# A planner's price list: changes of TensorE tile size, overlapping tiles and a shared port

## The chip, the cores and the metric

The kernel runs on one core of a Trainium2 chip. The metric is the device time of one execution in microseconds (us). Before the change three runs took 1749.36, 1751.22 and 1751.43 us. TensorE does matmuls (PE; its weight loads are PEld), VectorE (DVE), ScalarE (ACT) and GpSimd (POOL) work on elements, SyncE (SP) issues the DMAs that bring the weights.

## What is computed

A sequence of 256 tokens with 1024 features passes a first block and then a second block of two layers. In fp32, cut to what matters:

```
mod = silu(c) @ w_ada + b_ada                        # shift, scale and gate of a sublayer
h = rms_norm(x) * (1 + scale) + shift
first block, mixer:   p = h @ w_in
   y_a = rwkv7(r, decay, k, v, kk, a)                # 12 heads of 64: state' = state * w - (state kk)(kk a) + v k
   y_b = dilated window attention, three groups      # 12 heads of 64
   x += gate * rms_norm((sig(p_ga) * y_a @ w_a + sig(p_gb) * y_b @ w_b) @ w_out)
feed-forward:         x += gate * (silu(h @ w_u) * (h @ w_g)) @ w_o
second block, mixer (twice): compressed, selected and window attention (8 heads), forgetting
   attention (4 heads), attention within a block (4 heads), one output projection
order: mixer1, ffn, ffn, mixer2, ffn, ffn, mixer2, ffn, final norm
```

## The kernel before

**Dense products.** Features lie on the partitions, tokens on the free axis. A weight is loaded as fp32 in pieces of 128x1024 (`raw`), and split into two exact float32r parts: ACT writes `hi`, DVE writes `lo = raw - hi`. The operand is split alike (`hh`, `hl`). A product is three matmuls of 128x128 weights by 256 columns, hi by hh, hi by hl, lo by hh (`mm3`). These are the records `ps_mm<-hh,hi` and so on; a name `out<-a,b` gives the moving operand a and the stationary one b.

**Small products.** The mixers have plain fp32 matmuls with fewer than 128 rows or columns. They use a part of the array: 32x32, 64x64, 128x64 (128 rows, 64 columns), 64x128 or 128x32. An fp32 matmul is two records in the trace. In the first mixer, `rwkv` (L1653) treats two heads at a time, six pairs in three streams with PSUM tiles `ps_a`, `ps_b`, `ps_c`. A pair inverts small triangular blocks with 32x32 products (`block_inverse`, L1829), runs a chain over four chunks of 64 tokens (products `sv,am`, `rs,w`, `sv,c`, `bk,fbk`), and then adds up its output:

```
for n in range(4):
    for h in range(2):
        o = half[h]
        self.mm(py[o, 64 * n:64 * n + 64], sv[:, n, h], am[:, n, h, 1], n == 0, False)
        self.mm(py[o, 64 * n:64 * n + 64], uv[o, n, h], gb[o, n], False, True)
```

The first is the record pair `am,sv`, tile 128x64; the second is `gb,bk`, tile 64x64. Sums into `py` may change places, except that the first of a sum stays first. The norm of `py` follows, with products by exact matrices (`sph,exact`, `spl,exact`), then a gate. The attention (`attend`, L1962; `dilated`, L1613) has score products of 64 rows, transposes and value products of 64 columns.

**Order of the work.** The order is not written by hand. Each call of an engine in a stretch of the program only records an `_Op` with its operands and a duration (`time`, L641; `record`, L660; this helper is why all trace lines are L663). At the end of a stretch, `emit` (L836) plans: `solve` builds the dependencies, `run` (L423) simulates the engines and lets each take the ready instruction with the highest priority, `back` does it from the end to get new priorities, up to four times, and `replay` and `score` judge a plan by its mean end with eight shifts of the clock and noise. The best plan's order is emitted, and each engine keeps it, the DMA issues on SP too. Stretches are: the start (to about 97 us), the first mixer's projection and recurrence (97 to about 360), gates and dilated attention, the output projection, and then one for each feed-forward sublayer and each mixer of the second block.

For TensorE the plan has a price for each matmul, a factor of 2 while its own clock rule says slow, and a reserve: while a tick of that rule is short of columns, dense products go first. POOL and DVE are independent in the plan. The planning is done on the host while the program is built.

Of the kernel before, what the change touches and what calls it, by code (L numbers as in the profile page):

```python
# [25 lines left out]
D = 1024  # L26
# [10 lines left out]
# ---------------------------------------------------------------- host layout  # L37
def _pairs(w, chunks):
    """[K, N] -> [n pairs, 128, (K/128) * 256]: two 128-column chunks per pair, K-chunk major."""
    k = w.shape[0] // 128  # L40
    out = np.empty((len(chunks), 128, k, 256), w.dtype)
    for i, (a, b) in enumerate(chunks):
        out[i, :, :, :128] = w[:, a:a + 128].reshape(k, 128, 128).transpose(1, 0, 2)
        out[i, :, :, 128:] = w[:, b:b + 128].reshape(k, 128, 128).transpose(1, 0, 2)
    return out.reshape(len(chunks), 128, k * 256)


def _rows(w):
    """[K, N] -> [128, K/128, N]"""
    return np.ascontiguousarray(w.reshape(-1, 128, w.shape[1]).transpose(1, 0, 2))  # L50
# [22 lines left out]
# order of the 128-column chunks of the first block's projection  # L73
# [8 lines left out]
# units of the projection whose sums are all kept at a time  # L82
# [4 lines left out]
# order of the head dimensions of the first block's q and k: a rotated pair stays within 32 partitions  # L87
# [3 lines left out]
def _constants():  # L91
# [8 lines left out]
    # first block  # L100
# [60 lines left out]
def _pack(i):  # L161
    f = {k: np.asarray(v) for k, v in i.items()}
    o = {}
# [31 lines left out]
    # first block: six units whose K-chunks come first, then the others  # L195
# [21 lines left out]
    # second block  # L217
# [37 lines left out]
# ---------------------------------------------------------------- order of instructions  # L255
class _Op:
    """an instruction of a stretch of the program whose order is worked out before it is emitted"""
    __slots__ = ("eng", "emit", "cost", "lag", "cols", "tile", "pred", "succ", "prio", "behind", "where", "late", "side", "sums", "real", "start", "left", "ready", "num", "group", "banks")

    def __init__(self, eng, emit, cost, lag):  # L260
        self.eng, self.emit, self.cost, self.lag = eng, emit, cost, lag
        self.pred, self.behind, self.real, self.cols, self.tile, self.ready, self.sums, self.side = {}, [], None, 0.0, None, 0.0, False, False


class _Stretch:
    """the instructions of a stretch, by their dependencies and the times they take: each engine takes what is
    ready, the one with the longest way to the end first. Emission is in that order, and the engines keep it."""
    ENGINES = "pe", "act", "dve", "pool", "dma"
    # from the end of one engine's instruction to the start of another's that waits for it
    LAG = dict(zip(ENGINES, ((0.0, 0.2, 0.22, 0.22, 1.22), (0.24, 0.145, 0.145, 0.18, 1.22), (0.2, 0.13, 0.127, 0.2, 1.22),  # L270
                             (0.2, 0.08, 0.08, 0.1, 1.22), (0.95, 0.95, 0.95, 0.95, 0.0))))
    TICK, COLS = 10.24 / 3, float(2960)

    def __init__(self, model):
# [3 lines left out]
        self.state = dict(dict.fromkeys(self.ENGINES, 2.3), dma=1.69, queue=1.21), (0, 0.0, False, (0.0, None))  # L278
# [52 lines left out]
    def solve(self):  # L331
        ops = self.ops
        # a tile waits for the one whose place it takes
# [8 lines left out]
        # tiles of a ring start in turn  # L342
# [13 lines left out]
        # longest way to the end  # L356
# [13 lines left out]
    def tail(self, o):  # L370
        """us that an instruction without successors may come after the end"""
        return 20 if o.group == 12 else o.late

    def back(self, key):
        """the same from the end backwards: the times left to the end at which the instructions start"""
# [11 lines left out]
        while True:  # L387
# [22 lines left out]
            cost = o.cost  # L410
            if e == "pe":
                if o.side:
                    cost = 0.027
            free[e] = f = t + cost
# [8 lines left out]
    def run(self, prio, margin):  # L423
# [6 lines left out]
        ready = {e: [] for e in engines}        # by priority  # L430
        wait = {e: [] for e in engines}         # by time
        dense = []                              # those of the tensor engine that keep its clock up
# [7 lines left out]
        tick, cols, warm, last = self.state[1]  # L440
        while True:
            best = None
            for e in engines:
                w, t = wait[e], free[e]
                while w and w[0][0] <= t:
                    n = heappop(w)[1]
                    heappush(dense if rich[n] else ready[e], (prio[n], n))
                if not ready[e] and not (e == "pe" and dense):
                    if not w:
                        continue  # L450
                    t = w[0][0]
                if best is None or t < best[0]:
                    best = t, e
            if best is None:
                return end, out, (free, (tick, cols, warm, last))
            t, e = best
            w, r = wait[e], ready[e]
            if not r and not (e == "pe" and dense):
                while w and w[0][0] <= t:
                    n = heappop(w)[1]  # L460
                    heappush(dense if rich[n] else r, (prio[n], n))
            if e == "pe":
                k = int(t / self.TICK)
                if k != tick:
                    tick, warm, cols = k, k == tick + 1 and cols >= self.COLS, 0.0
                short = cols < target and ((k + 1) * self.TICK - t) * 2350 < target - cols + margin
                n = None
                if last[1] is not None and t < last[0] + 0.01 and r and 0:
                    # what the free rows or columns of the array can take at the same time
                    c = [x for x in r if ops[x[1]].tile is not None and not last[1] & ops[x[1]].tile]  # L470
                    if c:
                        c = min(c)
                        n = c[1]
                        r.remove(c)
                        heapify(r)
                if n is None:
                    n = heappop(dense if dense and (not r or short or dense[0] < r[0]) else r)[1]
            else:
                n = heappop(r)[1]
# [12 lines left out]
            if e == "pe":  # L492
                cols += o.cols
                if o.side:
                    cost = 0.027
# [6 lines left out]
            free[e] = f = t + cost  # L502
# [10 lines left out]
    def replay(self, order, phase, noise):  # L513
        """when a schedule ends if the windows of the tensor engine's clock lie otherwise and instructions take longer"""
        free, (tick, cols, warm, last) = dict(self.state[0]), self.state[1]
        tick, at, end = int((free["pe"] + phase) / self.TICK), [o.ready for o in self.ops], 0.0
        read = {}
        for _, n, o, _ in order:
# [7 lines left out]
            if e == "pe":  # L526
                k = int((t + phase) / self.TICK)
                if k != tick:
                    tick, warm, cols = k, k == tick + 1 and cols >= 2950.0, 0.0
                cols += o.cols  # L530
                if o.side:
                    cost = 0.027
                else:
# [1877 lines left out]
```

## Time and profile before

| | |
|---|---|
| three runs, us | 1749.36, 1751.22, 1751.43 (median 1751.22) |
| span of the profiled execution, first to last instruction | 1749.4 us |
| time of the runs beyond that span (median less span) | 1.8 us |
| PE busy | 1658.9 us, 95% of the span |
| DVE, ACT, POOL busy | 1274.3, 910.0, 409.5 us |
| mean granted clock of TensorE | 0.969 of full speed |

The time of the profiled execution itself is its span and what little lies around it; the runs were timed apart from it. In the tables of stretches each line gives the length, then for each engine its busy time and in brackets its instructions, then PEclk, the granted TensorE clock (1.00 is 2.4 GHz, 0.50 is 1.2 GHz), the DMA share and the GB/s. A busy PE is not PE at its peak: a product may hold it long.

### The profile page before, as it was taken

The numbers are of one execution on the slowest core, as the hardware profiler recorded it, in microseconds if no ns is written. First come the engines' busy times: TensorE is split into PE (matmuls) and PEld (weight loads), VectorE is DVE, ScalarE is ACT, GpSimd is POOL, SyncE is SP. The second block draws the span as 40 slices with busy tenths as digits, with TensorE's granted clock in tenths as the row PEclk, the third lists the DMA queues.
The fourth block names the chain that finished last, engine by engine and source line by source line (L and its number), as shares of the span: only waits on it lengthen the run. The fifth ranks groups of instructions, "written<-read, shape, count | busy, mean of one in ns | idle before, by whom it ended". The sixth has DMA issues, their size and how long they took to land.

```text
span 1749.4 us, 35779 instructions
## 1 busy us (share of the span) xinstructions
PE 1658.9 (95%) x14110; PEld 1545.0 (88%) x14110; DVE 1274.3 (73%) x2389; ACT 910.0 (52%) x1707; POOL 409.5 (23%) x486
## 2 busy tenths in 40 slices
PE   5888988999999999999999999999999989999998
PEld 4877777788899999999878799999999977799997
DVE  5697476358877789878787877777777786775553
ACT  4464364357644446454566564545444556565442
POOL 3475053013500024000433330004000414440002
PEclk9989979899999999999999999999999999899999
DMA  9433324235588885878751568896888752245553
GB/s 352 170 123 122 110 75 168 91 127 185 191 274 290 298 294 193 298 276 311 254 177 61 174 201 294 278 309 212 275 293 294 278 194 88 73 157 182 193 181 97
DMA packets 102554, 359.18 MB, mean 205 GB/s; under 512 B 11377, under 2 KB 12913, under 8 KB 102386
## 3 DMA queue, kind: packets, MB, share of 16 engines
q1 hardware_dynamic: 102386, 356.90, 59.9%
q8 instruction: 110, 1.80, 0.4%
q14 instruction: 58, 0.48, 0.1%
HBM read 355.81 MB, written 1.05 MB: 204 GB/s over the span
## 4 chain that ended last, share of the span: by engine, by line
PE 74%; DVE 9%; POOL 4%; issue 2%; ACT 2%; DMA 2%; DVEq 0%; POOLq 0%; SPq 0%; ACTq 0%
PE ps_mm L663 57%; PE ps_a L663 9%; PE ps_b L663 5%; PE ps_c L663 4%; DVE lo L663 3%; POOL fg L663 2%; DMA raw<-in_ada 1%; DVE junk L663 1%; ACT hi L663 1%; DMA w<-in_cw 1%; DVE x L663 0%; DVE rt L663 0%; DVE am L663 0%; ACT w L663 0%; POOL P1a L663 0%
## 5 line engine op out<-in xcount | busy, mean ns | idle before, releaser
L663 DVE TENSOR_TENSOR lo<-raw,hi 128x1024 fp32r<-128x1024 f32 (+2 forms) x478 | 579.8, 1233 | 186.4 <-issue 67.3
L663 ACT ACTIVATE hi<-raw 128x1024 fp32r<-128x1024 f32 (+2 forms) x478 | 487.4, 1025 | 362.2 <-PE ps_mm L663 267.5
L663 PE MATMUL ps_mm<-hh,hi 128*128 128x256 f32 x2040 | 514.7, 289 | 30.0 <-ACT hh L663 18.2
L663 PE MATMUL ps_mm<-hl,hi 128*128 128x256 f32 x2040 | 506.7, 287 | 0.5 <-DVE hl L663 0.4
L663 PEld LDWEIGHTS ps_mm<-hh,hi 128*128 128x128 f32 x2040 | 389.2, 194 | 41.5 <-ACT hh L663 21.2
L663 PEld LDWEIGHTS ps_mm<-hl,hi 128*128 128x128 f32 x2040 | 388.4, 194 | 5.3 <-issue 2.5
L663 PE MATMUL ps_mm<-hh,lo 128*128 128x256 f32 x2040 | 319.3, 285 | 0.7 <-DVE lo L663 0.7
L663 DVE CUSTOM_DVE_ANT_0 junk<-raw,cond 128x1024 bf16<-128x1024 f32 x192 | 241.4, 1257 | 65.3 <-DMA raw<-in_ada 64.0
L663 PEld LDWEIGHTS ps_mm<-hh,lo 128*128 128x128 f32 x2040 | 275.5, 192 | 4.5 <-DVE lo L663 1.3
L663 POOL TENSOR_TENSOR acc<-acc,sq 128x256 f32<-128x256 f32 x46 | 49.7, 1080 | 864.8 <-ACT sq L663 863.2
L663 PE MATMUL ps_mm<-fh,hi 128*128 128x256 f32 x770 | 189.5, 282 | 0.1
L663 PEld LDWEIGHTS ps_mm<-fh,hi 128*128 128x128 f32 x770 | 146.4, 191 | 1.1 <-DVE fy L663 1.1
L663 PE MATMUL ps_mm<-fl,hi 128*128 128x256 f32 x490 | 120.8, 281 | 0.0
L663 PE MATMUL ps_mm<-fh,lo 128*128 128x256 f32 x770 | 115.8, 281 | 0.0
L663 PEld LDWEIGHTS ps_mm<-fh,lo 128*128 128x128 f32 x770 | 102.7, 191 | 0.0
L663 PEld LDWEIGHTS ps_mm<-fl,hi 128*128 128x128 f32 x490 | 93.3, 190 | 0.0
L663 ACT ACTIVATE fh<-fy 128x256 fp32r<-128x256 f32 x110 | 44.9, 411 | 58.7 <-DVE fy L663 58.7
L663 PE MATMUL ps_mm<-fg,hi 128*128 128x256 f32 x280 | 69.7, 281 | 0.0
L663 ACT ACTIVATE su<-ps_mm 128x256 f32<-128x256 f32 x95 | 36.0, 379 | 59.5 <-PE ps_mm L663 59.4
L663 PE MATMUL ps_a<-UH,hi 128*128 128x258 f32 x168 | 50.7, 305 | 4.4 <-ACT UH L663 4.4
L663 ACT ACTIVATE UH<-x,mod 128x256 fp32r<-128x256 f32 x56 | 27.7, 504 | 49.8 <-DVE x L663 49.8
L663 PEld LDWEIGHTS ps_mm<-fg,hi 128*128 128x128 f32 x280 | 53.4, 191 | 0.0
(575 smaller groups left out, 3029.7 us busy)
## 6 DMA issues: line engine op xcount, KB each, us to landing
raw<-in_ffi SPq DMA_DIRECT2D x220, 512.0 KB, 5.0
raw<-in_ada SPq DMA_DIRECT2D x192, 512.0 KB, 5.2
raw<-in_ffo SPq DMA_DIRECT2D x100, 512.0 KB, 5.1
raw<-in_win SPq DMA_DIRECT2D x66, 512.0 KB, 4.4
raw<-in_wout SPq DMA_DIRECT2D x24, 512.0 KB, 3.9
w<-in_cw SPq DMA_DIRECT2D x16, 512.0 KB, 8.1
raw<-in_ws SPq DMA_DIRECT2D x16, 448.0 KB, 7.7
raw<-in_ffo SPq DMA_DIRECT2D x20, 256.0 KB, 4.1
```

What stands on the lines that cost most here:

```text
L663: emit = lambda: f(*a, **k)
```

## The change

All in the planner, besides comments taken out of the file. What `record` and `time` say of a TensorE instruction changes: its tile size (`mode`), which of 16 subarrays it uses (`subs`), its passes (`pas`: two for fp32), a pass's time `d`, and `hold`, how long it keeps the engine from issuing. In `run`, `replay` and `back` a new method `issue` then gives the start and the end: after a change of size it waits for all before it and 0.095 us more; at the same size only for its own subarrays. Ready products are kept in one heap for each size, a change of size is handicapped by `stay`, and among small ones of a size one whose subarrays are free is preferred. `emit` plans with five values of `stay` and keeps the best. The clock rule has one level for becoming fast and another for staying so, and the reserve's floor is lower. DVE instructions with two SBUF tensors and POOL instructions with one exclude one another (`port`, `lock`).

```
-    TICK, COLS = 10.24 / 3, float(2960)
+    TICK, COLS = 10.24 / 3, (2950.0, 2350.0)
+    SWITCH = 0.095
+    def issue(self, o, t, pe, slow):
+        mode, ends, full = pe
+        if o.mode != mode:
+            t = max(t, full + self.SWITCH)
+        else:
+            for i in o.subs:
+                if ends[i] > t:
+                    t = ends[i]
+        d = o.d * slow
+        f = t + o.pas * d
+        for i in o.subs:
+            ends[i] = f
+        pe[0], pe[2] = o.mode, max(full, f)
+        return t, f if len(o.subs) == 16 else f - d + 0.005, f
# run(self, prio, margin, stay=0.0)
-        target = 3300
+        target = 2900
-        rich = [o.eng == "pe" and o.tile is None and o.cols > 2000 * o.cost for o in ops]
+        kind = [None if o.eng == "pe" and o.mode == (128, 128) and o.cols > 2000 * o.cost else o.mode for o in ops]
-                    n = heappop(dense if dense and (not r or short or dense[0] < r[0]) else r)[1]
+                for x, h in modes.items():
+                    if h:
+                        p = h[0][0] + (0.0 if pe[0] == (x or (128, 128)) else stay) - (1e6 if short and x is None else 0.0)
+                        if c is None or p < c[0]:
+                            c = p, x
...
+                if ops[n].subs is not ALL and h and pe[0] == ops[n].mode:
+                    took, kept = (max(pe[1][i] for i in ops[n].subs), (p, n)), []
+                    while h and h[0][0] < p + 0.5 and len(kept) < 8 and took[0] > t + 0.01:
...
-                if o.side:
-                    cost = 0.027
-                    last = t + cost, (last[1] or 0) | o.tile
-                else:
-                    if o.tile is None and last[1] is not None:
-                        cost += 70 / 1000
-                    cost *= 1 if warm else 2
-                    last = t + cost, o.tile
-            free[e] = f = t + cost
+                t, free[e], f = self.issue(o, t, pe, 1 if warm else 2)
+            else:
+                if o.port:
+                    t = max(t, lock[other[e]])
+                    lock[e] = t + cost
+                free[e] = f = t + cost
# time(self, op, out, ins, kw), TensorE; n moving columns, m stationary ones
-                return 2 * (n / 2400.0 + 0.0025)
+                return 2 * n / 2400.0 + 0.002
-                return n / 2400.0 + 0.0025
-            return 4 * max(n / 2400.0 + 0.0025, 0.025)
+                return n / 2400.0 + 0.0115
+            return 2 * max(2 * n / 2400.0 + 0.002, m / 1200.0 + 0.003 if m == 128 else 0.0)
# record
+            x.pas = 1 if ins[1].dtype == F32R or k.get("is_transpose") else 2
+            x.d = x.hold = x.cost / x.pas
+            size = lambda n: 32 if n <= 32 else 64 if n <= 64 else 128
+            x.mode = size(rows), size(cols)
-                x.side = c0 > 0
...
+                x.hold = (x.pas - 1) * x.d + 0.007
+        elif self.name in ("dve", "pool"):
+            x.port = sum(1 for a in ins if a.space == SBUF and a.free_size() > 1) > (self.name == "dve")
# emit
-        new = rec.run([-o.prio for o in ops], margin)
-        new += (rec.score(new),)
-        best = improve(new, new)
+        best = None
+        for stay in (0.0, 0.4, 1.2, 3.0, 8.0):
+            new = rec.run([-o.prio for o in ops], margin, stay)
+            new += (rec.score(new),)
+            if best is None or new[3] < best[3]:
+                best = new
+            best = improve(new, best, stay)
```

`replay` has the same edits as `run`, and `back` uses `hold` for the engine and the full duration for who waits.

## Rows read from the trace of the kernel before

**Rows 1.** the page's busy times and its chain by engine

```profile
PE 1658.9 (95%) x14110; PEld 1545.0 (88%) x14110; DVE 1274.3 (73%) x2389; ACT 910.0 (52%) x1707; POOL 409.5 (23%) x486
PE 74%; DVE 9%; POOL 4%; issue 2%; ACT 2%; DMA 2%; DVEq 0%; POOLq 0%; SPq 0%; ACTq 0%
```

**Rows 2.** table of stretches: length, busy time and instructions of each engine, clock, DMA

```profile
97.00:250.00 153.00, 133.35 (x1529) 112.66 (x1529) 108.61 (x214) 74.69 (x189) 64.52 (x72) 0.87 0.33 105
250.00:360.00 110.00, 105.60 (x1413) 90.56 (x1413) 62.77 (x131) 43.86 (x115) 26.46 (x26) 0.89 0.34 112
655.00:850.00 195.00, 193.88 (x1597) 192.41 (x1596) 159.70 (x245) 102.09 (x153) 28.31 (x31) 0.99 0.77 264
850.00:1005.00 155.00, 147.22 (x1069) 123.09 (x1067) 127.00 (x383) 96.43 (x250) 56.30 (x86) 1.00 0.47 160
1390.00:1551.00 161.00, 153.31 (x1074) 127.00 (x1073) 124.20 (x375) 96.98 (x250) 60.93 (x88) 0.96 0.41 140
```

**Rows 3.** the same table for four short stretches of the first mixer

```profile
204.30:217.00 12.70, 12.70 (x92) 9.10 (x91) 3.14 (x8) 1.76 (x7) 0.58 (x4) 0.81 0.14 44
217.00:225.00 8.00, 8.00 (x34) 5.63 (x35) 0.80 (x2) 1.46 (x4) 0.29 (x2) 0.50 0.01 2
331.00:338.00 7.00, 7.00 (x59) 5.52 (x58) 3.32 (x7) 1.88 (x5) 0.00 (x0) 1.00 0.52 183
338.00:350.00 12.00, 12.00 (x60) 8.95 (x60) 1.02 (x4) 1.62 (x5) 0.00 (x0) 0.52 0.01 3
```

**Rows 4.** timeline of PE: start, length, instruction, number; warm and cold

```profile
208.43 0.33 PE L663 MATMUL ps_a<-am,sv 128*64 128x64 f32 x2
208.69 0.33 PE L663 MATMUL ps_a<-gb,bk 64*64 64x64 f32 x2
208.95 0.33 PE L663 MATMUL ps_a<-am,sv 128*64 128x64 f32 x2
...
214.03 0.47 PE L663 MATMUL ps_b<-am,sv 128*64 128x64 f32 x2
214.44 0.47 PE L663 MATMUL ps_b<-gb,bk 64*64 64x64 f32 x2
```

**Rows 5.** timeline of PE, some us earlier

```profile
204.12 0.34 PE L663 MATMUL ps_b<-sv,am 128*64 128x64 f32 x4
204.28 0.29 PE L663 MATMUL ps_c<-sv,am 128*64 128x64 f32 x4
204.40 0.28 PE L663 MATMUL ps_a<-am,sv 128*64 128x64 f32 x2
204.61 0.32 PE L663 MATMUL ps_a<-gb,bk 64*64 64x64 f32 x2
```

**Rows 6.** PE groups by shape, one of three alike: busy us, mean ns

```profile
L663 PE MATMUL ps_a<-am,sv 128*64 128x64 f32 x32 | 5.2, 244 | 0.0
```

**Rows 7.** timeline of PE: after the first and the last of 551 changes

```profile
11.70 1.22 PE L663 MATMUL ps_c<-acc,c 128*128 128x256 f32 x2 [0.60 <-DVE acc L663]
...
1531.22 0.61 PE L663 MATMUL ps_mm<-oh,lo 128*128 128x256 f32 x3
```

**Rows 8.** timeline of PE: a row of 64x64 and one of 32x32 products

```profile
140.02 0.96 PE L663 MATMUL ps_b<-c,rkv 64*64 64x64 f32 x16
140.91 1.21 PE L663 MATMUL ps_mm<-hh,lo 128*128 128x256 f32 x8
...
144.11 0.45 PE L663 MATMUL ps_c<-w,t 32*32 32x32 f32 x32 [0.22 <-ACT w L663]
```

**Rows 9.** POOL: one tile's shortest, median and longest; one group's mean

```profile
L663 POOL TENSOR_TENSOR U<-w,ct x6: 477/1032/3046, 138.4 to 274.6; 128x128 f32<-128x128 f32 x6
...
L663 POOL TENSOR_TENSOR fg<-fg,rstd 128x256 f32<-128x256 f32 x40 | 45.3, 1167 | 8.8 <-ACT rstd L663 8.8
```

**Rows 10.** table of stretches, the first mixer's first 40 us

```profile
97.00:137.00 40.00, 31.89 (x200) 29.21 (x200) 38.43 (x65) 21.60 (x49) 30.83 (x31) 0.83 0.29 94
```

More of the change, by code (lines that the diff above doesn't have):

```diff
@@ L250, in _pack @@
     return {k: np.ascontiguousarray(a) for k, a in o.items()}, v.at
+ALL = range(16)
 class _Op:
-    __slots__ = ("eng", "emit", "cost", "lag", "cols", "tile", "pred", "succ", "prio", "behind", "where", "late", "side", "sums", "real", "start", "left", "ready", "num", "group", "banks")
+    __slots__ = ("eng", "emit", "cost", "lag", "cols", "tile", "pred", "succ", "prio", "behind", "where", "late", "side", "sums", "real", "start", "left", "ready", "num", "group", "banks", "mode", "subs", "pas", "d", "hold", "port")
     def __init__(self, eng, emit, cost, lag):
@@ L262, in __init__ @@
         self.pred, self.behind, self.real, self.cols, self.tile, self.ready, self.sums, self.side = {}, [], None, 0.0, None, 0.0, False, False
+        self.mode, self.subs, self.pas, self.d, self.hold, self.port = (128, 128), ALL, 1, cost, cost, False
 class _Stretch:
@@ L409, in back @@
             o = ops[n]
-            cost = o.cost
-            if e == "pe":
-                if o.side:
-                    cost = 0.027
-            free[e] = f = t + cost
+            free[e] = t + o.hold
+            f = t + o.cost
             out[n] = f
@@ L439, in run, with admit @@
         out, end, read = [], 0.0, {}
-        tick, cols, warm, last = self.state[1]
+        tick, cols, warm, pe = self.state[1]
+        pe = [pe[0], list(pe[1]), pe[2]]
+        lock = dict(self.state[2])
+        other = dict(dve="pool", pool="dve")
+        npe = 0
+        def admit(e, t):
+            nonlocal npe
+            w = wait[e]
+            while w and w[0][0] <= t:
+                n = heappop(w)[1]
+                if e == "pe":
+                    heappush(modes.setdefault(kind[n], []), (prio[n], n))
+                    npe += 1
+                else:
+                    heappush(ready[e], (prio[n], n))
         while True:
@@ L443, in run @@
             for e in engines:
[L444 to L449, printed above, removed]
+                t = free[e]
+                admit(e, t)
+                if not (npe if e == "pe" else ready[e]):
+                    if not wait[e]:
                         continue
-                    t = w[0][0]
+                    t = wait[e][0][0]
                 if best is None or t < best[0]:
@@ L454, in run @@
             if best is None:
-                return end, out, (free, (tick, cols, warm, last))
+                return end, out, (free, (tick, cols, warm, (pe[0], tuple(pe[1]), pe[2])), lock)
             t, e = best
[L457 to L461, printed above, removed]
+            admit(e, t)
             if e == "pe":
@@ L513, in replay @@
     def replay(self, order, phase, noise):
[L515 removed]
+        free, (tick, cols, warm, pe) = dict(self.state[0]), self.state[1]
+        pe = [pe[0], list(pe[1]), pe[2]]
+        lock = dict(self.state[2])
+        other = dict(dve="pool", pool="dve")
         tick, at, end = int((free["pe"] + phase) / self.TICK), [o.ready for o in self.ops], 0.0
@@ L528, in replay @@
                 if k != tick:
-                    tick, warm, cols = k, k == tick + 1 and cols >= 2950.0, 0.0
+                    tick, warm, cols = k, k == tick + 1 and cols >= self.COLS[warm], 0.0
                 cols += o.cols
-                if o.side:
-                    cost = 0.027
-                else:
-                    if o.tile is None and last[1] is not None:
-                        cost += 70 / 1000
-                    cost *= 1 if warm else 2
-                last = t, o.tile
-            free[e] = f = t + cost
+                t, free[e], f = self.issue(o, t, pe, 1 if warm else 2)
+            else:
+                if o.port:
+                    t = max(t, lock[other[e]])
+                    lock[e] = t + cost
+                free[e] = f = t + cost
             for b in o.banks:
@@ L843, in emit, with improve @@
         pass
-        def improve(new, best):
+        def improve(new, best, stay):
             for it in range(4):
@@ L850, in improve @@
                 left = rec.back([-f for f in fin])
-                old, new = new, rec.run([-f for f in left], margin)
+                old, new = new, rec.run([-f for f in left], margin, stay)
                 if new[0] < best[0] + 5.0:
```

54 lines of the change are left out of this document (26 added, 28 removed).

## The prediction

> **What bounds the kernel now.** The page comes first: TensorE is busy for 95% of the 1749.4 us span and carries 74% of the chain that ended last, POOL carries 4% of it, about 70 us, and POOL's whole busy time is 23% of the span [rows 1]. That says the tensor engine, but not where it wastes time, so the table of stages is next [rows 2]. A feed-forward stretch is a wall of matmuls: 193.88 of 195 us, clock 0.99, and a better order has next to nothing to win there. The first block's mixer (97 to 360 us) is different: 239 of 263 us busy, but at a clock of 0.87 and 0.89, with 2942 matmul records. The two mixers of the second block are the same code twice, 155 us at clock 1.00 and 161 us at 0.96; their busy shares are both 95%.
>
> The third view is the table of two short stretches of the first mixer [rows 3]. From 204.3 to 225 us, and again from 331 to 350, PE is busy without a gap while DVE, ACT and POOL are almost idle. Between 217 and 225 us it gets through 34 records in 8 us. Nobody feeds it slowly there; it is slow by itself. The timeline shows why [rows 4]. The output products of the recurrence come as one product `am,sv` (two records, tile 128x64), then one `gb,bk` (two records, 64x64), and so on: each start is 0.26 us behind the last at full clock and 0.40 us behind at the half clock. The same kind of product, when products of one tile size follow one another, costs far less [rows 5]: ten records start between 204.12 and 204.61 us, with one change of size at the end.
>
> **The change, part by part.** The planner decides the order of every engine's instructions; the device runs no instruction more or less.
>
> *1. Alternating products.* Before, the planner charges a small fp32 product 0.117 us, or 0.027 us when its output starts above partition 0, and never charges a change between two small sizes. The pair at 0.26 us a product is thus booked at 0.027 to 0.117. After, a change costs 0.095 us in the plan, and of five weights for staying with a size the best is kept. How many: `ps_a<-am,sv` has 32 records [rows 6]; with three banks and two products of this kind that is 6 x 32 = 192 records, 96 products. About half run at either clock: the stretches of [rows 3] have PEclk 0.81, 0.50, 1.00 and 0.52. So they take 48 x 0.256 + 48 x 0.403 = 31.6 us now. Grouped, from [rows 5]: 0.49 us less one change of 0.095 is 0.040 us a record, 0.080 a product, 7.7 us for 96; add two changes for each of six pairs of heads, 1.1 us. That is 8.8 us at full clock, 16.5 if it all ran at half. The saving lies between 15 and 23 us, zero if the order stayed. I take 20, nearer to the full clock, at which the first part of each alternation runs now too. It lies on the path one for one, because in [rows 3] no other engine has work. The products add to one sum and may change places, only the first of a sum is fixed, so no data forbid the grouping. After it comes, as the next late thing, the norm of the recurrence's output (`sph`, `exact`), which follows as a chain through ACT and DVE, with dense projection products to cover it.
>
> *2. The other changes of size.* Along PE's timeline the tile size changes 551 times; the first and the last are in [rows 7]. About 100 are those of part 1. The price of one is the plan's 0.095 at least; at most it is what the alternating product costs beyond its own two records. Sixteen records of 64x64 in a row take 0.89 us up to the next start [rows 8], less a change 0.050 each, so that is 0.256 - 2 x 0.050 = 0.156. All 450 others are 43 us at the lower price, which I take. Most are forced: a step of a head's chain needs its own size, and the next dense product another. I take a fifth, 90 x 0.095 = 8.6 us, at the 95% by which PE is on the path in these stages 8 us; bounds 0 and two fifths, 17 us.
>
> *3. The port.* POOL instructions are slow when DVE works beside them: `U` (128x128) takes 477 ns at best and 3046 at worst, `fg<-fg,rstd` 1167 on average [rows 9]. The new plan lets a POOL instruction and a DVE instruction with two SBUF operands exclude one another, so it sees these waits and can place POOL work elsewhere. POOL's 4% of the chain are 70 us; if a twentieth of it went, 3 us. It can also go the other way, DVE being held in the plan for POOL: the first 40 us of the mixer have DVE busy for 38.43 [rows 10], and where it is shifted there, the whole chain waits. Bounds: 10 us gained, 10 lost; I take 3 gained.
>
> *4. Dense prices and the clock rule.* A dense product of 256 columns is booked at 0.118 instead of 0.109 us, the plan's rule for its clock gets two levels in place of one, and the floor below which dense products are pulled ahead falls from 3300 to 2900. In the feed-forward stretches nothing can come of this: PE has 1.1 us of idle time in 195 [rows 2]. In the mixers it lets small products go first more often. I take zero, bounds 3 gained and, apart from the rival below, 3 lost.
>
> No wait is added to the program; what is added is order. A product held back for its size holds the PE queue's successors only in the plan, but its consumer really waits: ACT's copy of `ps_a`, then the next product of that head. DMA issues on SP are moved with the plan as well; their share in the first mixer is 0.33, so a transfer some us later still lands in time [rows 2].
>
> Sum: 20 + 8 + 3 + 0 = 31 us off a span of 1749.4. The three timed runs have a median of 1751.2, 1.8 us above the span, which I carry along: 1751.2 - 31 = 1720. All terms at their ends together would give 15 + 0 - 10 - 3 = 2 to 23 + 17 + 10 + 3 = 53 us off; they will not all lie at one end, and the forecast's own range is 9 to 49 off, 1702 to 1742.
>
> In the Trainium skill, "TensorEngine Tiling (Array Packing)", section "Restrictions and Gotchas", different row tiles can't access the same PSUM bank at one time. By that rule the grouped `gb,bk` of a pair's two halves, which go to one bank, would not overlap, and each of the 96 records of it would cost 0.050 us as in the row at 140.02 instead of 0.040: the saving of part 1 would be 1 us less and the time 1721. The trace speaks against it: 32 records of 32x32 tiles, four row tiles into the one bank `ps_c`, last 0.45 us together [rows 8], 14 ns each.
>
> **The rivals.**
> *A. Much faster.* With true prices the whole first mixer may be packed anew. At clocks 0.87 and 0.89 a quarter of its time is at half speed, 64 us, which costs up to 32; its idle PE time is 24 us [rows 2]. Were half of each gained beside the 31, 31 + 16 + 12 = 59 less 8 counted twice gives 51: 1700. For it: DVE's 171 us in 263 leave room. Against: at the beginning of each half DVE is the bound [rows 10].
> *B. Nothing comes of it.* The alternation comes from equal priorities; a plan with weight 0 for staying may win and keep it, or the freed time may end as a wait for the chain of norms. Then part 1 gives 0 to 5 and parts 2 and 3 what they give at least: 1743 to 1753. Against: the price now makes the alternating order 17 us worse in the plan itself.
> *C. Slower: the clock.* Dense products are kept in reserve less, so small ones gather and TensorE falls to 1.2 GHz in more places. The price is read from the twin mixers: 0.04 of clock is 6 us [rows 2]. If both of the second block's mixers fell to the first's 0.87, that is 13 and 9 hundredths, 20 + 14 = 34 us against the 31 gained: 1754; if the first mixer lost half as much again, 1771. It decides from a mean clock of about 0.88 in the second block's mixers. For it: the cold stretches of [rows 3] are just those filled with small products, and grouping fills more such. Against: these two mixers run at 1.00 and 0.96 although they hold small products already, and a grouped run is over sooner.
>
> **How the numbers follow.** The forecast (1702 to 1742) gets 0.58, A (below 1702) 0.14, B (1742 to 1755) 0.14, C (above 1755) 0.14. A fifth of all may lie outside: I leave out C and the far half of A, so the range is 1690 to 1756. A measurement of this kernel tells 0.2%, 3.5 us, from no change: faster is below 1747.7, the forecast, A and nearly half of B, 0.78; the same 0.08; slower 0.14.
>
> **What would show it.** Part 1 is right if `am,sv` and `gb,bk` no longer take turns on PE, and their 192 records together hold PE for about 9 to 16 us. Part 2 shows in the count of size changes: about 550 - 100 - 90 = 360. Part 3 shows in a lower mean of `fg<-fg,rstd` and of POOL's busy time for the same 486 instructions. Part 4: feed-forward stretches within 3 us of before. The first mixer (97 to 360 us) should be about 25 us shorter and hold nearly all of the gain; were the gain mostly in the feed-forward stretches, or the mixers' clock lower with the time still down, my reasons would be wrong even at the right time. The prediction fails if the two stretches of [rows 3] keep their 20 us each.

## The result, and the profile after

The changed kernel takes 1710.78 us (median of four runs, 1703.46 to 1714.97) against 1751.33; the ratio is 0.9766, interval 0.9738 to 0.9793. Forecast were 1720 and a range of 1690 to 1756. The profiled execution took 1711.47 us, its span is 1709.7. So the time is right within 10 us; of its four terms one is right, one did not come, one was ten times too small, and the fourth, zero, is not contradicted.

First the page of after: busy times, and the chain that ended last by engine; they answer to [rows 1].

```profile
PE 1632.1 (95%) x14110; PEld 1523.0 (89%) x14110; DVE 1272.0 (74%) x2389; ACT 907.1 (53%) x1707; POOL 389.9 (23%) x486
PE 79%; DVE 9%; ACT 4%; DMA 4%; issue 3%; POOL 1%; SPq 0%; DVEq 0%; ACTq 0%; POOLq 0%
```

The instructions are the same in number. PE is busy 26.8 us less, and idle (span less busy) 77.6 us in place of 90.5, 12.9 less: that is the whole 39.7 us of the spans. To see where, the table of stretches is cut at marks in the program, since fixed times no longer mean the same work: the start up to the last of its `tp,va` products, the first mixer up to a sum-of-squares product (`ps_c<-sq,c`) ahead of the first feed-forward, and the two mixers of the second block. Columns as in [rows 2]. Before:

```profile
0.00:98.90 98.90, 72.84 (x469) 64.77 (x470) 64.77 (x108) 48.26 (x85) 39.91 (x51) 0.95 0.72 257
98.90:442.40 343.50, 314.80 (x3515) 270.93 (x3515) 228.48 (x457) 166.42 (x392) 115.90 (x121) 0.91 0.38 125
850.70:1009.70 159.00, 151.13 (x1096) 126.70 (x1095) 129.61 (x384) 99.48 (x252) 60.30 (x90) 1.00 0.48 161
1390.60:1555.30 164.70, 157.01 (x1101) 130.59 (x1101) 126.12 (x375) 99.97 (x252) 64.63 (x92) 0.96 0.40 137
```

After:

```profile
0.00:88.70 88.70, 67.55 (x464) 61.10 (x464) 63.73 (x105) 47.37 (x82) 37.33 (x50) 0.98 0.77 285
88.70:413.40 324.70, 297.05 (x3521) 259.99 (x3520) 230.48 (x461) 167.99 (x395) 110.68 (x122) 0.89 0.42 135
821.00:981.30 160.30, 157.15 (x1115) 127.97 (x1114) 130.72 (x384) 99.71 (x253) 64.15 (x93) 1.00 0.47 159
1361.40:1517.80 156.40, 150.98 (x1108) 126.81 (x1107) 123.57 (x375) 100.30 (x253) 63.97 (x95) 0.99 0.43 145
```

The start is 10.2 us shorter and the first mixer 18.8. What follows gives 10.7, mostly the last of these mixers (8.3). The five feed-forward stretches change by -2.3 to +1.3 us.

In the first mixer the alternation of [rows 4] is gone. PE's timeline of after (start, length, instruction, number), two places of it:

```profile
203.86 0.56 PE L705 MATMUL ps_a<-gb,bk 64*64 64x64 f32 x11
...
204.46 0.51 PE L705 MATMUL ps_a<-am,sv 128*64 128x64 f32 x10
...
205.89 0.56 PE L705 MATMUL ps_b<-am,sv 128*64 128x64 f32 x10
206.38 0.27 PE L705 MATMUL ps_b<-gb,bk 64*64 64x64 f32 x1
206.38 0.27 PE L705 MATMUL ps_a<-gb,bk 64*64 64x64 f32 x1
```

Ten records now start within 0.49 us, up to the next size, where before four needed 0.52. All 192 records hold PE for 8.9 us from each start to the next, all at full clock; before it was 30.7 (12.3 at full clock, 18.4 at half). The group that answers to [rows 6] takes 2.3 us for 5.2:

```profile
L705 PE MATMUL ps_a<-am,sv 128*64 128x64 f32 x32 | 2.3, 228 | 0.0
```

The tile size changes 479 times instead of 551, and between `am,sv` and `gb,bk` 7 times instead of 86. One thing got worse: a long stretch at the half clock. It stands in two lines of the table of stretches, in order of time the second first:

```profile
233.60:274.60 41.00, 39.43 (x254) 33.98 (x258) 29.03 (x48) 15.37 (x32) 16.78 (x18) 0.50 0.41 129
224.00:233.60 9.60, 6.84 (x54) 6.36 (x53) 9.16 (x14) 5.89 (x11) 8.79 (x12) 1.00 0.01 4
```

Ahead of it PE had 54 records in 9.6 us and stood still for 2.8 of them. At half the clock there is work for 39.43 of 41 us. Before, the two longest such stretches had 17.1 and 13.7 us, those of the alternation. All stretches at the half clock together are 109 us before and 89 after.

### The profile page after: what moved, and what is told of

Read it like the earlier page. It is cut to its first block, busy times and chain, and to the rows that moved or that the text cites. A ratio compares the mean times of both kernels' runs of the same rounds, so it can differ in the third digit from the quotient of the medians.

```text
span 1709.7 us, 35805 instructions
## 1 busy us (share of the span) xinstructions
PE 1632.1 (95%) x14110; PEld 1523.0 (89%) x14110; DVE 1272.0 (74%) x2389; ACT 907.1 (53%) x1707; POOL 389.9 (23%) x486
## 4 chain that ended last, share of the span: by engine, by line
PE 79%; DVE 9%; ACT 4%; DMA 4%; issue 3%; POOL 1%; SPq 0%; DVEq 0%; ACTq 0%; POOLq 0%
PE ps_mm L705 59%; PE ps_a L705 10%; PE ps_b L705 6%; PE ps_c L705 4%; DVE lo L705 3%; DMA raw<-in_ada 1%; ACT hi L705 1%; DVE x L705 1%; DMA w<-in_cw 1%; DVE junk L705 1%; POOL mod L705 1%; DMA raw<-in_ffi 1%; POOL nrm L705 0%; DVE am L705 0%; DVE fy L705 0%
## 5 line engine op out<-in xcount | busy, mean ns | idle before, releaser
L705 DVE TENSOR_TENSOR lo<-raw,hi 128x1024 fp32r<-128x1024 f32 (+2 forms) x478 | 573.8, 1221 | 207.1 <-issue 73.9
L705 POOL TENSOR_TENSOR acc<-acc,sq 128x256 f32<-128x256 f32 x46 | 46.2, 1005 | 856.4 <-ACT sq L705 854.9
L705 ACT ACTIVATE su<-ps_mm 128x256 f32<-128x256 f32 x95 | 35.5, 374 | 28.1 <-PE ps_mm L705 28.1
```

Of the source, the lines that this page charges most:

```text
L705: emit = lambda: f(*a, **k)
```

## The experiments

Twelve kernels were run, in three groups, each beside the kernel before (medians 1748.04, 1750.01 and 1748.65 us). The table gathers them; busy and idle of PE and the changes of tile size are of the profiled execution. That of e1 was the fastest of its four (the median is 6.5 us longer), that of e10 the slowest (5.7 us above the median). The kernel after was not timed again in these groups. Differences to it are given between medians; by the ratios to before they are 38 us for e3, 6 for e4, 13 for e8 and 19 for e9, where the medians give 34, 9, 14 and 21.

| kernel | median us | ratio to before, interval | span | PE busy | PE idle | changes |
|---|---|---|---|---|---|---|
| before | 1751.3 | 1 | 1749.4 | 1658.9 | 90.5 | 551 |
| after | 1710.8 | 0.9766, 0.9738 to 0.9793 | 1709.7 | 1632.1 | 77.6 | 479 |
| e1 before, grouped | 1729.8 | 0.9888, 0.9859 to 0.9917 | 1721.5 | 1631.3 | 90.2 | 483 |
| e2 after, turns forced | 1708.9 | 0.9767, 0.9741 to 0.9793 | 1712.0 | 1625.9 | 86.1 | 461 |
| e3 after, no port | 1744.5 | 0.9984, 0.9957 to 1.001 | 1740.6 | 1631.4 | 109.2 | 437 |
| e4 after, old clock rule | 1701.6 | 0.9729, 0.9711 to 0.9747 | 1700.1 | 1615.7 | 84.4 | 410 |
| e5 before, port | 1755.2 | 1.0028, 1.0013 to 1.0044 | 1753.4 | 1670.5 | 82.9 | 624 |
| e6 before, grouped, port | 1726.9 | 0.9886, 0.985 to 0.9922 | 1722.2 | 1629.2 | 93.0 | 517 |
| e7 after, no port, old clock rule | 1746.4 | 0.9975, 0.9957 to 0.9992 | 1737.7 | 1618.5 | 119.2 | 356 |
| e8 after, second choice | 1696.5 | 0.9694, 0.9671 to 0.9717 | 1693.7 | 1614.6 | 79.1 | 408 |
| e9 after, third choice | 1689.9 | 0.9659, 0.9643 to 0.9676 | 1689.3 | 1610.9 | 78.4 | 405 |
| e10 after, no weight for staying | 1734.0 | 0.991, 0.989 to 0.993 | 1737.8 | 1660.6 | 77.2 | 627 |
| e11 old clock rule, second choice | 1701.9 | 0.9737, 0.9698 to 0.9776 | 1695.8 | 1612.8 | 83.0 | 426 |
| e12 no port, third choice | 1760.3 | 1.0063, 1.0044 to 1.0082 | 1757.8 | 1644.2 | 113.6 | 409 |

### e1: the grouping alone, in the kernel before

```
         for n in range(4):
             for h in range(2):
                 o = half[h]
                 self.mm(py[o, 64 * n:64 * n + 64], sv[:, n, h], am[:, n, h, 1], n == 0, False)
+        for n in range(4):
+            for h in range(2):
+                o = half[h]
                 self.mm(py[o, 64 * n:64 * n + 64], uv[o, n, h], gb[o, n], False, True)
```

Expected:

> The planner of before; only the loop that records the recurrence's output products is cut in two, first all am,sv, then all gb,bk, so that equal priorities no longer alternate them. Theory (the alternation itself is the largest term): am,sv and gb,bk together hold PE for 9 to 16 us instead of 31, the first mixer ends 15 to 20 us earlier, and the time is 1731 to 1736. Rival (the gain is the new planner's packing as a whole): the 20 us come back as waits or dense work elsewhere, 1746 to 1751.

Three added lines give 1.1%, 19.6 us by the ratio (18.2 between the medians). The 192 records take 8.8 us, as in after, and PE's idle time stays at 90: everything is busy time, 27.6 us less, of which the 192 records have 21.9. The size of part 1 is shown, without a new planner. The first mixer of this kernel (columns as above):

```profile
98.70:414.10 315.40, 289.59 (x3513) 253.17 (x3513) 228.10 (x457) 166.44 (x391) 110.21 (x120) 0.93 0.41 136
```

That is 28.1 us less than before, and 9.3 less than in after: in this place the three lines do better than the changed planner with the plan that it chose.

### e2: the changed planner, with the turns forced

```
+        prev = None
...
-                self.mm(py[o, 64 * n:64 * n + 64], sv[:, n, h], am[:, n, h, 1], n == 0, False)
-                self.mm(py[o, 64 * n:64 * n + 64], uv[o, n, h], gb[o, n], False, True)
+                for x in ((sv[:, n, h], am[:, n, h, 1], n == 0, False), (uv[o, n, h], gb[o, n], False, True)):
+                    ins = self.mm(py[o, 64 * n:64 * n + 64], *x)
+                    if prev is not None:
+                        self.after(ins, prev)
+                    prev = ins
```

Expected:

> The planner of after, with edges that force am,sv and gb,bk to take turns as before. Theory: PE pays the 20 us again, 1727 to 1733, nearly all of it before the second sublayer. Rival (the new planner would hide it under other engines' work): 1711 to 1716.

The theory of this run fell: nothing was lost. The time is near the rival's, but nothing had to be hidden. PE's timeline shows how the planner gets round the order that is forced on each pair of heads:

```profile
203.64 0.27 PE L705 MATMUL ps_a<-am,sv 128*64 128x64 f32 x1
203.65 0.27 PE L705 MATMUL ps_b<-am,sv 128*64 128x64 f32 x1
203.75 0.22 PE L705 MATMUL ps_a<-am,sv 128*64 128x64 f32 x1
203.75 0.22 PE L705 MATMUL ps_b<-am,sv 128*64 128x64 f32 x1
203.81 0.28 PE L705 MATMUL ps_c<-am,sv 128*64 128x64 f32 x2
204.02 0.27 PE L705 MATMUL ps_a<-gb,bk 64*64 64x64 f32 x1
```

It takes the same step of three pairs together: three products in 0.38 us, one change for the three. The 192 records take 13.6 us. So it is not the freedom to reorder one sum that ends the loss, but the planner's new account of tile sizes. Whether in it the price of a change does that, or the heaps by size, or the overlaps, was not taken apart.

### e3: the changed kernel without the port

```
-            x.port = sum(1 for a in ins if a.space == SBUF and a.free_size() > 1) > (self.name == "dve")
+            pass
```

Expected:

> After, with DVE and POOL independent in the plan again. Theory (the port is a small term): 3 us slower, 1711 to 1717, POOL's busy time back from 390 towards 409 us. Rival (the port carries what the first mixer does not explain, the 8 us of the last second-block mixer and the 10 us at the start): 1722 to 1730.

34 us are lost, nearly the whole gain, where 3 were expected and the rival allowed 22 to 30 (1722 to 1730 is its range, 1744.5 was measured); the kernel can't be told from the one before any more. PE is as little busy as in after and the 192 records take 8.4 us; but its idle time goes to 109.2 us, 19 above the kernel before. The longest waits of PE, first without the port (us in total, times, longest):

```profile
PE ps_mm L705 <- DVE fy L705: 15.6, 13, 2.5
PE ps_mm L705 <- ACT hh L705: 14.6, 8, 5.4
PE ps_a L705 <- DVE bk L705: 12.5, 2, 7.9
...
PE ps_b L705 <- POOL P0b L705: 6.7, 7, 2.3
```

and in after:

```profile
PE ps_mm L705 <- ACT rz L705: 12.1, 4, 5.8
PE ps_mm L705 <- ACT hh L705: 10.8, 6, 5.4
...
PE ps_mm L705 <- DVE fy L705: 3.8, 8, 0.6
PE ps_a L705 <- DVE bk L705: 3.5, 1, 3.5
```

What comes late without the port is what DVE and POOL make: `fy` 15.6 against 3.8 us, `bk` 12.5 against 3.5, and `P0b` is not among the seven longest waits of after. The first mixer is no part of the loss, it is 12.9 us shorter than in after. The start is 10.4 us longer and the two mixers of the second block 8.3 and 9.6 (columns as above):

```profile
0.00:99.10 99.10, 72.55 (x471) 63.17 (x472) 69.46 (x114) 48.89 (x85) 44.07 (x53) 0.94 0.76 269
99.10:410.90 311.80, 287.57 (x3513) 249.39 (x3512) 225.63 (x451) 165.25 (x391) 114.13 (x119) 0.95 0.42 137
823.80:992.40 168.60, 156.82 (x1122) 129.89 (x1121) 127.77 (x384) 100.86 (x253) 65.03 (x93) 0.96 0.47 156
1380.70:1546.70 166.00, 154.09 (x1121) 127.96 (x1120) 125.49 (x375) 99.96 (x253) 63.49 (x92) 0.99 0.42 138
```

PE stands idle for 11.8 and 11.9 us in these mixers; in after it is 3.2 and 5.4, before 7.9 and 7.7. The feed-forward stretches lose as well, 15.5 us together, and 14.5 of the 31.6 us of added idle time lie there. One of them, first in after and then without the port, with the same work for PE:

```profile
981.30:1175.60 194.30, 192.05 (x1593) 189.96 (x1592) 148.24 (x220) 97.52 (x141) 21.48 (x22) 1.00 0.78 271
992.40:1190.40 198.00, 192.29 (x1591) 189.88 (x1590) 148.04 (x220) 98.48 (x141) 21.64 (x21) 1.00 0.76 261
```

### e4: the changed kernel with the clock rule of before

```
-    TICK, COLS = 10.24 / 3, (2950.0, 2350.0)
+    TICK, COLS = 10.24 / 3, (2960.0, 2960.0)
-        target = 2900
+        target = 3300
```

Expected:

> After, with one level in the plan's clock rule (2960) and the reserve's floor at 3300, as before. Theory (the lower floor let TensorE stay at half clock from 233.6 to 274.6 us, which costs up to 20 us): that stretch goes or shrinks below 15 us, 1695 to 1704. Rival (the levels are what let small products go first and so gave part of the gain): 1716 to 1725.

It is 9 us faster than after, as this theory said (6 by the ratios, whose intervals just overlap), and the 41 us stretch at the half clock breaks up into three of at most 10.2 us. That stretch is not all of it: of the 9.6 us between the spans 4.6 lie in the first mixer and 4.8 in the two later ones. Whether the rule did this, or only another plan, e11 tests.

### e5 and e6: the port alone in the kernel before, and with the grouping

The port's lines of after (`port`, `lock`) are put into the old `run`, `replay` and `record`; for e6 the two loops of e1 as well.

```
+            if o.port:
+                t = max(t, lock[other[e]])
+                lock[e] = t + cost
             free[e] = f = t + cost
```

Expected:

> The kernel before with the port alone: in its own planner (old prices of TensorE, old clock rule) DVE instructions with two SBUF tensors and POOL instructions with one exclude one another. Nothing else is edited, so the products am,sv and gb,bk should go on taking turns (about 30 us on PE). Theory: the port pays by itself, because the plan sees the waits between DVE and POOL, and is worth about what was lost when it alone was taken out of the changed kernel (34 us): 1748 - 34 = 1714, bounds 1705 to 1726, with the idle time of PE in each mixer of the second block falling from 13 us to 7 to 9. Rival 1: the port only repairs what the new TensorE prices spoil after the first mixer (23 us there without it); then it is worth 0 to 11 us here, 1737 to 1750, and PE's idle time in these mixers stays at 11 to 14 us. Rival 2 (the prediction's size): 3 us, 1745, within the same bounds.

> The kernel before with the two loops of the grouping experiment (all am,sv first, then all gb,bk) and the port in the old planner. Theory: the two savings lie in different places (the grouping in the first mixer, the port mostly after it) and add: 20 us by the grouping and 34 by the port, 1748 - 54 = 1694, bounds 1685 to 1706; then neither the new prices nor the new clock rule is needed for the time of the changed kernel. Rival: the port repairs only, and grouping and port give 20 + 0 to 11 us: 1717 to 1729. Between 1706 and 1717 the port is worth 11 to 23 us and both are partly right.

Both theories fell. The port alone makes the kernel slower by 0.3%, above the ranges of the theory and of both rivals; beside the grouping it adds nothing to e1 that can be told apart (1726.9 and 1729.8, the intervals overlap), as the rival there said. The page's busy times say where the time of e5 went:

```profile
PE 1670.5 (95%) x14110; PEld 1547.1 (88%) x14110; DVE 1274.2 (73%) x2389; ACT 908.8 (52%) x1707; POOL 400.3 (23%) x486
```

Idle time of PE falls by 7.6 us, the start is as short as in after (86.0 us), but busy time rises by 11.6, with 73 more changes of tile size. This planner prices only one kind of them, a dense product behind a small one, at 0.07 us: 241 of its 624. Also the 192 records take 33.8 us instead of 30.7, as more of them run at the half clock. In e6 the start has 4.5 us less idle time than in e1, but three of the feed-forward stretches have 2 to 4 more each, and I can't say why. In both kernels the feed-forward after the first of the second block's mixers takes 204 us instead of 193, 6 of it by idle time of PE (6.7 instead of 0.8); which part of the plan makes it so stays open too. Each of these is one plan of the old planner, whose spread over other choices was not tried; that the port is not worth 34 us in it is shown, a loss of 5 us is not.

### e7: without the port, and with the old clock rule

This is e3 and e4 in one.

> The changed kernel without the port and with the clock rule and the floor of before (one level of 2960, floor 3300); prices and overlaps of TensorE stay new. It tells whether the 23 us that the kernel without the port lost after the first mixer come from the clock rule or from TensorE's new prices. If from the clock rule: 1744 - 23 = 1721, bounds 1712 to 1728, the sublayers after the first mixer within 5 us of before in sum. If from the prices (small products dearer, so that dense ones are planned at other places): only the 9 us that the old rule gave in the changed kernel come, 1735, bounds 1730 to 1746, the sublayers after the first mixer 12 or more above before.

1746.4, at the upper end of what was expected if the prices lose it: the loss of e3 does not come from the clock rule. Beside e4, which differs by the port alone, 45 us are lost. Of 14 kernels this one has the fewest changes of tile size, 356, and the most idle time of PE, 119.2 us. Few changes alone do not make PE wait, though: e9 below has 405 and 78.4 us of idle time, e12 has 409 and 113.6.

### e8 and e9: other choices of the plan

The score that picks among plans uses random numbers; here they start elsewhere.

```
-        rng = np.random.RandomState(0)
+        rng = np.random.RandomState(1)          # e9: 2
```

Expected:

> The changed kernel with other random numbers in the score that picks among the plans (seed 1 in place of 0). Nothing of the model changes, so this is what the choice of a plan moves by itself. Theory: little, 1711 within 6 us (1705 to 1717), so that the port's 34 us and the grouping's 20 stand well above it. Rival: the planner is fickle, and another choice moves the time by 15 us or more (below 1696 or above 1726); then single experiments with the planner do not tell causes apart.

> The changed kernel with a third choice of plan (random numbers of the score from seed 2). So far the two choices gave 1711 and 1697 us. Theory: the change's gain is in the model and any choice keeps most of it: 1704, within 1692 to 1716, PE busy 1610 to 1635 us, PE idle in the span 75 to 85 us, am,sv and gb,bk at 9 to 14 us. Rival: the gain hangs on the choice of plan, and this one lies at 1720 or above.

The choice moves the time by 14 and 21 us: both theories were too narrow, and in e8 the rival lay nearer. But all three plans are far below the kernel before, and e9 is the fastest kernel of this study, 0.9659. Its marked stretches:

```profile
0.00:89.20 89.20, 68.28 (x463) 62.12 (x464) 63.14 (x104) 46.78 (x81) 39.62 (x50) 0.96 0.76 282
89.20:403.20 314.00, 282.60 (x3521) 247.91 (x3520) 231.28 (x462) 168.49 (x397) 115.37 (x122) 0.94 0.42 140
811.10:967.40 156.30, 151.10 (x1120) 128.01 (x1119) 130.43 (x384) 100.61 (x253) 67.13 (x94) 0.99 0.49 167
1346.40:1497.90 151.50, 149.44 (x1110) 125.64 (x1108) 122.94 (x375) 100.83 (x253) 66.33 (x94) 1.00 0.43 150
```

The first mixer is 10.7 us shorter than in after, at a clock of 0.94 against 0.89: there is no stretch at the half clock of over 10.2 us. It is as long as in e1 (315.4), so what the changed planner adds to the three lines by hand lies outside the first mixer. The two later mixers are 4 and 5 us shorter, with 75 and 83 changes of size where after has 119 and 89.

### e10: no weight for staying with a size

```
-        for stay in (0.0, 0.4, 1.2, 3.0, 8.0):
+        for stay in (0.0,):
```

Expected:

> The changed kernel planned with the weight 0 for staying with a tile size alone (in place of the best of 0, 0.4, 1.2, 3 and 8). Theory: the grouping of am,sv and gb,bk comes from the price of a change in the plan's time and from the heaps by size together with priorities worked out from priced plans, the weight only adds to it: the 192 records stay at 9 to 14 us, the other changes of size rise from 450 by up to 60, PE busy 1632 to 1645, time 1706 to 1722. Rival: the weight makes the grouping; without it products of equal priority take turns again, the 192 records take 25 us or more and the time is 1725 to 1740.

The mechanism is the theory's, the time the rival's. The 192 records stay grouped (10.7 us), so it is not the weight that groups them. But the other changes rise: 627 in all, 148 more than in after and 76 more than before. PE's busy time rises by 28.5 us while its idle time is that of after. In this plan, without the weight, the new prices bring fewer changes nowhere but in the recurrence's output. The 23 us above after are hardly more than what another choice of plan moves (14 and 21 us); the 148 changes are well beyond it (405 to 479 in three choices).

### e11: the old clock rule with the second choice of plan

Both edits, that of e4 and that of e8.

> The changed kernel with the clock rule and floor of before and, beside it, the second choice of plan (seed 1). With the first choice the old rule was 9 us better (1702 against 1711), with the new rule the second choice was 14 us better (1697 against 1711). Theory: the 9 us were one 41 us stretch at the half clock which that one plan had; the plan of the second choice has no such stretch, so the rule matters little here: 1698, within 1693 to 1704. Rival: the old rule is worth some 9 us in any plan, 1688, within 1682 to 1692, and this is the fastest kernel of all.

1701.9 against 1696.5 of e8: here the old rule is no gain, rather 5 us of loss, within overlapping intervals. The 9 us of e4 are a matter of the one plan. That the clock rule is worth anything by itself is not shown.

### e12: no port, the third choice of plan

> The changed kernel without the port, with the third choice of plan (seed 2); with the first choice it took 1744 us, and 1746 with the old clock rule, and PE was idle for 109 and 119 us of the span against 78 and 79 in the two plans with the port. Theory: the new TensorE prices without the port make plans in which PE waits for DVE and POOL, whatever the choice: PE idle 100 to 122 us, time 1736 to 1752. Rival: those were two unlucky plans; idle time below 92 us and a time of 1705 to 1728.

1760.3 us, 70 above e9, which has the port and the same random numbers. Idle time is 113.6 us, inside the theory's bounds; the time is worse than they allow, since PE's busy time is up too (1644.2) and the half clock holds for 136 us. With the random numbers of e8 the planner without the port comes to the very order of e3, so the pair is 1744.5 and 1696.5. With the old clock rule e7 and e4 are a further pair, 1746.4 and 1701.6. Three choices with the port: PE idle 77.6 to 79.1 us (77 to 86 in the plans of e2, e4, e10 and e11, which have it too). Three plans without (e3, e7, e12): 109.2 to 119.2. The port's effect in this planner stands well above the fickleness of the choice.

## Why the prediction was right, and where it was wrong

*Part 1, alternating products: right.* 20 us were forecast, 21.8 came on PE (30.7 to 8.9, forecast 9 to 16 left), and e1 gives 19.6 on the chip by the grouping alone. That it lies on the path nearly one for one is shown by e1 too: no other engine took the place. The Trainium skill's rule that was weighed there ("TensorEngine Tiling (Array Packing)", section "Restrictions and Gotchas": different row tiles don't reach one PSUM bank at a time) is not seen here either: the 192 records with all their changes average 0.047 us, and the eleven `gb,bk` in one bank, which must be of both halves since each half has eight, take 0.49 us up to the next size, where eleven at 0.050 would need 0.55 before any change.

*Part 2, the other changes of size: wrong.* I took a fifth of 450 away, about 360 left in all; after has 479, and the 72 that went are those of the alternation: where neither product is an `am,sv` or `gb,bk` there are 453 changes before and 451 after. The step that failed is "I take a fifth", which stood on no row. Its reason is argued only: the plan may also spend a change where that fills PE, and e10 shows that without a weight it spends more of them than before. There may have been something to be had: e8, e9 and e4 have 405 to 410 changes and 16 to 21 us less busy time. But they also stand at the half clock for 14 to 28 us less than after, so how much of it the changes are is not shown. In the plan that after came with, it isn't had.

*Part 3, the port: the mis-sized term.* 3 us forecast, within 10 either way. Taking it out of after costs 34 us, 45 with the old clock rule and 70 with the third choice. I sized it by POOL's share of the chain (4%, 70 us, now 1%), that is by what POOL itself held up. What it removes is PE's waiting for results of DVE and POOL, `fy` and `bk` above all. In the kernel before these two waits are 2.1 and 7.7 us. So the port wins some of the wait for `bk`, and for `fy` it makes good what the new prices without it spoil. And I added the parts up as if each were worth the same alone. They aren't: prices without the port are worth 4 us (e3; -12 with the third choice, e12), the port without the prices -5 (e5), both 41; the first three differ from nothing by less than a choice of plan moves. Each makes the other's loss good: prices alone leave PE waiting longer (109 against 90 us), the port alone makes more changes of size (624 against 551). My signs for it were poor too: `fg<-fg,rstd` has a mean of 1063 ns in after, less than the 1167 of [rows 9], but 959 in e3 without the port, and POOL's busy time, 389.9 us for 409.5, is 392.9 in e7 without the port and 402.5 in e9 with it. So it is shown that PE waits less in plans with the port. That fewer DVE and POOL instructions hold one another up is not shown, and no run asks whether longer times for them in the plan would do as well. Why the prices without the port raise idle time above that of before is argued only: a plan that books PE's small products as overlapping expects DVE and POOL to keep up with it.

*Part 4, dense prices and clock rule: zero, and no sign is shown* for the clock rule (the old one gives -9 us with one plan, +5 with another and +2 without the port: e4, e11, e7). The dense prices were not taken out by themselves. Feed-forward stretches within 3 us: right.

*The place.* The first mixer was to be 25 us shorter and hold nearly all the gain. Up to the first feed-forward 29.0 of 39.7 us are won, but 10.2 of them in the start, which I had not looked at: it takes 86 to 92 us in the plans with the port and 96 to 99 in those without, with old prices or new: this part goes with the port alone. The mixer itself gives 18.8, less than its 21.8 on the alternation, as the 41 us at the half clock take some back: e1 and e9, which have no such stretch, give 28.1 and 29.5 there. That is rival C at work, in one place and at a lower price: its clock goes from 0.91 to 0.89, not that of the later mixers. A lower clock with the time down was my own sign of wrong reasons; for part 1 e1 answers it, for the rest of this mixer the sign stands. Rival A's size, 1700 and below, is what e8 and e9 reach.

So the sum came right in part by luck. By PE's own account the 39.7 us are 21.8 of part 1, 5.0 of other busy time, and 12.9 of idle time, where the forecast has 20, 8 and 3: too much in part 2 stands against too little for the port.

## What to carry to other kernels

When a planner writes the order, price what the hardware charges in all its forms together: a model that is truer in one term only may bring nothing or a little loss, as the halves did here (e3, e7, e12 and e5, from 0.3% gained to 0.6% lost). Compare such changes over a few choices of plan before one believes a difference of 1%, and split the span into the bound engine's busy and idle time: each half of this change, taken alone, bettered one of them and worsened the other (e3 and e5). And a pattern seen in the timeline, like two tile sizes taking turns, may be worth three lines by hand first: that was half of the gain, and nearly all that any plan here won in the place where the pattern stood.

## What the runs showed of the hardware

A dense product of 256 columns that follows a dense one starts 0.120 us ahead of the next (median of some 9300 at full clock in after). Where the first of the two stands behind a small product it is 0.223 (median of 98), 0.103 more. The change costs something on its other sides too: the first dense product starts 0.152 us behind the last record of 128x64 (22), where two such records in a row lie 0.051 apart (254), and the first 128x64 record starts 0.211 behind a dense product (10) in place of 0.120. Added up, going from dense to small products and back costs some 0.3 us at full clock, 0.15 a change; that is an estimate from these medians. Between after and e10, 148 more changes go with 28.5 us more busy time, 0.19 each; the plans differ in more than that, so this is a sign of the same size and no price.

Three products of one size can share one change though they go to three PSUM banks: in e2 they (six records) take 0.38 us including a change, where one took 0.26 before.
